# Sums of squares amid the first k chunk, an earlier fetch of the exponential's table, turns by twos and closer spatial products in a two-layer decoder trunk

## Chip, cores and metric

The kernel runs on one core of a Trainium2 chip. The metric is the device time of one execution in microseconds (us). The kernel before takes 947.1 us, the median of three runs (946.36 to 947.19).

## The reference, cut to what matters

Two layers work on 256 tokens of width 1024, in fp32. Each layer adds half of a gated feed-forward (width 2816), then a mixer, then half of a second feed-forward; every one of these starts from an RMS norm. The first layer's mixer runs dilated window attention (8 heads of 64) beside a gated spatial product (4 groups of 128), and the second layer's is causal attention with 16 heads (256 tokens are one block, so no other block is chosen).

```python
def rms_norm(x, g):
    xf = x.astype(jnp.float32)
    y = xf * lax.rsqrt(jnp.mean(xf * xf, axis=-1, keepdims=True) + EPS)
    return (y * g.astype(jnp.float32)).astype(x.dtype)

def chunked_spatial_gating(u, v, v_norm_g, w_s, b_s):
    u = jax.nn.gelu(u)
    v = rms_norm(jax.nn.gelu(v), v_norm_g)
    ...
    mixed = jnp.einsum('gpq,bnqgc->bnpgc', ws, v) + jnp.swapaxes(b_s, 0, 1)[None, None, :, :, None]
    return (u * mixed).reshape(b, s, g * c)

    # reference()
    for layer in range(DEPTH):
        h = h + 0.5 * swiglu(rms_norm(h, ffn1_norm[layer]), ...)
        hn = rms_norm(h, mix_norm[layer])
        h = h + (ab_mixer(hn, ...) if layer % 2 == 0 else c_mixer(hn, ...))
        h = h + 0.5 * swiglu(rms_norm(h, ffn2_norm[layer]), ...)
    return rms_norm(h, final_norm)
```

## The kernel before

Activations lie transposed in SBUF: features on the partitions, the 256 tokens along the row. Every product is made of three matmuls on reduced-precision operands (`mm3`, lines 223 to 226): each fp32 operand is split into a high half, written by ScalarE (`whi`, line 105; `split`, line 229), and a low half, the difference, written by VectorE (`wlo`, line 106; line 230). The matmuls are high by high (L224), high by low (L225) and low by high (L226).

Weights stream in chunks of 1 MB. `Stream` loads them over SyncE's queue into three raw buffers and splits them into four pairs of split buffers, so splits run up to four chunks ahead of TensorE. `take` hands out the next chunk, `free` gives its buffers back and starts the next loads and splits. The instructions of each engine are put in order when the program is built, by a scheduler that sees the order of the Python code; on TensorE that order is nearly the code's.

A stage doesn't wait for its norm: its matmuls run on values without the factor 1/rms, and this factor is put on behind them. `Next.pair` (lines 265 to 290) collects the squares of the new activations with VectorE adds into `acc`; `Next.sums` (line 291) adds them over the partitions with four small TensorE matmuls against ones (L295) and takes the mean (`ms`, L297, VectorE) and the root (`rstd`, L233, GpSimd). `Next.spread` turns the factor into a row that all partitions hold: two wide copies on ScalarE (L310), two TensorE instructions (L312, L313) and two copies (`row`, `half`).

Both mixers start with `first_tiles` (line 752). Its q chunk makes two tiles of 128 columns, `ps4[0]` and `ps4[1]`, with their last two k at the end; then come the sums, then the k chunk's two tiles, then the spread. `put_q` and `put_k` scale these tiles by the row and split them. The scores of two heads that lie in one tile of 128 partitions use operands of which one half of the partitions is zero (`ql0` to `ql3`); `make_attention` clears those with one memset of `zeros` (L628) and casts of it on GpSimd (L633).

Attention of a head has three parts. `scores` (line 667) runs four matmuls (L676, L677), VectorE's masked minimum (L680), the exponential on ScalarE (L683), the reciprocal of its sum (L686) and the scaling of the probabilities (L690, on GpSimd, for the last four heads on VectorE). `turn` transposes the probabilities with three TensorE instructions (L698) and splits them; `weighted` multiplies two heads by v. These parts and the spatial products (`mixing`, with a two-buffered `tmp`) are hung into the stream of weight tiles by `Slots`: `step()` is called after each tile and runs what stands at that slot. In the first mixer slots 0 to 3 are the first tiles, 4 to 7 v, 8 to 11 the gate's v, 12 to 15 its u, 16 to 19 the last q and k tiles, 20 to 27 the output projection. In the second 0 to 3 are the first tiles, and the projection has 24 to 31.

ScalarE holds one table of functions at a time. The program loads the exponential's where the exponentials of L683 follow other functions; the first mixer also needs one for the gate's gelu (L822, L859).

Of the kernel before, what the change touches and what calls it, by code (L numbers as in the profile page):

```python
# [10 lines left out]
F32 = mybir.dt.float32  # L11
F32R = mybir.dt.float32r
AF = mybir.ActivationFunctionType
ALU = mybir.AluOpType

S = 256
D = 1024
NT = S // 128
KD = D // 128
# [12 lines left out]
LINE, SHIFT = 64, 16  # L32
# [110 lines left out]
def trunk(ctx: ExitStack, tc: tile.TileContext, a, out):  # L143
    nc = tc.nc
# [3 lines left out]
    wk = ctx.enter_context(tc.tile_pool(name="wk", bufs=2))  # L148
# [10 lines left out]
    st = Stream(nc, (raw_pool, hi_pool, lo_pool))  # L159
# [463 lines left out]
    def make_attention(mp, mask_cols, nheads, v, mix, rows=False):  # L623

        qs, ks, probs, pts = {}, {}, {}, {}
        pairs, flying = (4, 5) if rows else (2, 4)
        zeros = mp.tile([128, S], F32, name="zeros")
        nc.gpsimd.memset(zeros, 0.0)  # L628
        seconds = [mp.tile([128, 2 * S + LINE], F32R, name=f"ql{i}") for i in range(pairs)]
        for t in seconds:  # L630
            for j in range(2):
                o = slice(64 - j * 64, 128 - j * 64)
                nc.gpsimd.tensor_copy(t[o, SHIFT + j * S : SHIFT + (j + 1) * S], zeros[o, :])  # L633
        mask = mp.tile([128, 384], F32, name="mask")
        nc.scalar.dma_start(mask, a["consts"][:, mask_cols])

        def scaled(bk):
            t = mp.tile([128, S], F32, name="qk", bufs=3)
            nc.vector.tensor_mul(t, bk[:, :S], norm["row"])
            return t  # L640

        def sides(j):
            return slice(j * 64, j * 64 + 64), slice(64 - j * 64, 128 - j * 64)

        def put_q(p, bk):

            t = bk[:, :S] if rows else scaled(bk)
            qq = mp.tile([128, 2 * S + LINE], F32R, name="q", bufs=pairs)
            for j in range(2):
                q, ql = (u[:, SHIFT + j * S : SHIFT + (j + 1) * S] for u in (qq, seconds[p % pairs]))  # L650
                r, o = sides(j)
                nc.scalar.activation(q[r, :], t[r, :], AF.Copy)
                nc.vector.tensor_sub(ql[r, :], t[r, :], q[r, :].bitcast(F32))
                nc.gpsimd.tensor_copy(q[o, :], q[r, :].bitcast(F32))
                qs[2 * p + j] = (q, ql)

        def put_k(p, bk):

            t = scaled(bk)
            for j in range(2):  # L660
                k = mp.tile([128, S], F32R, name=f"k{j}", bufs=pairs)
                r, o = sides(j)
                nc.scalar.activation(k[r, :], t[r, :], AF.Copy)
                nc.gpsimd.tensor_sub(k[o, :], t[r, :], k[r, :].bitcast(F32))
                ks[2 * p + j] = k

        def scores(h):
            q, ql = qs.pop(h)
            k = ks.pop(h)
            sc = bank()  # L670
            pr = mp.tile([128, 384], F32, name="pr", bufs=flying)
            nm = wk.tile([128, 2], F32, name="nm")
            l = wk.tile([128, 2], F32, name="l")
            for b in range(2):
                bs = slice(b * 128, b * 128 + 128)
                nc.tensor.matmul(sc[:, b * S : (b + 1) * S], q[:, bs], k, start=True, stop=False)  # L676
                nc.tensor.matmul(sc[:, b * S : (b + 1) * S], ql[:, bs], k, start=False, stop=True)  # L677
            for b, (c0, n) in enumerate(((0, 128), (128, 256))):
                cs = slice(c0, c0 + n)
                nc.vector.tensor_tensor_reduce(pr[:, cs], sc[:, b * S : b * S + n], mask[:, cs],  # L680
                                               norm["score"][:, b : b + 1] if rows else -SCALE, 3e38,
                                               op0=ALU.add, op1=ALU.min, accum_out=nm[:, b : b + 1])
                nc.scalar.activation(pr[:, cs], pr[:, cs], AF.Exp, bias=nm[:, b : b + 1], scale=-1.0,  # L683
                                     accum_out=l[:, b : b + 1])
            rl = wk.tile([128, 2], F32, name="rl")
            nc.vector.reciprocal(rl, l)  # L686
            for b, (c0, n) in enumerate(((0, 128), (128, 256))):
                cs = slice(c0, c0 + n)
                engine = nc.gpsimd if h < nheads - 4 else nc.vector
                engine.tensor_scalar(pr[:, cs], pr[:, cs], rl[:, b : b + 1], None, op0=ALU.mult)  # L690
            probs[h] = pr

        def turn(h):
            p, j = divmod(h, 2)
            pr = probs.pop(h)
            tp = bank()
            for i in range(3):
                nc.tensor.transpose(tp[:, i * 128 : (i + 1) * 128], pr[:, i * 128 : (i + 1) * 128], ident)  # L698
            if j == 0:
                pts[p] = [mp.tile([128, 2, 384], F32R, name=n, bufs=2) for n in ("pth", "ptl")]  # L700
            split(pts[p][0][:, j, :], pts[p][1][:, j, :], tp[:, :384])

        def weighted(p):
            o = bank().rearrange("p (j c) -> p j c", j=2)
            pth, ptl = pts.pop(p)
            vs = slice(p * 128, (p + 1) * 128)
            mm3(o, v[0][:, 0, vs], v[1][:, 0, vs], pth[:, :, :256], ptl[:, :, :256], True, False)
            mm3(o[:, :, 128:], v[0][:, 1, vs], v[1][:, 1, vs], pth[:, :, 256:], ptl[:, :, 256:], False, True)
            for j in range(2):
                r = slice(j * 64, j * 64 + 64)  # L710
                split(mix[0][r, p], mix[1][r, p], o[r, j, :].rearrange("p (t c) -> p t c", t=NT))

        return put_q, put_k, scores, turn, weighted
# [7 lines left out]
    class Slots:  # L721
# [9 lines left out]
        def step(self, *_):  # L731
            for f, i in self.events.pop(self.now, []):
                f(i)
            self.now += 1

    def tile_of(p, w, j, ks=range(KD)):

        cs = slice(j * 128, (j + 1) * 128)
        for k in ks:
            mm3(p[:, :S], w[0][k][:, cs], w[1][k][:, cs], xT["h"][:, k], xT["l"][:, k], k == 0, k == KD - 1)  # L740
# [11 lines left out]
    def first_tiles(put_q, put_k, step):  # L752

        ps4 = [bank() for _ in range(4)]
        w = st.take()
        for j, ks in LATE:
            tile_of(ps4[j], w, j, ks)
        for _ in range(2):
            step()
        st.free()  # L760
        nxt.sums()
        w = st.take()
        for j in range(2):
            tile_of(ps4[2 + j], w, j)
            step()
        nxt.spread()
        norm["score"] = wk.tile([128, NT], F32, name="score", bufs=1)
        nc.vector.tensor_scalar(norm["score"], norm["col"], -SCALE, None, op0=ALU.mult)
        for j in range(2):
            put_q(j, ps4[j])  # L770
            put_k(j, ps4[2 + j])
        st.free()
# [23 lines left out]
    def ab_mixer(phase):  # L796
        with tc.tile_pool(name="mp", bufs=1) as mp:
# [4 lines left out]
            put_q, put_k, scores, turn, weighted = make_attention(mp, slice(0, 384), 8, v, mix)  # L802
# [46 lines left out]

            slots = Slots()  # L850
            slots.at((9,), lambda _: turn_spatial())
            slots.at((15, 16, 17, 18), mixing)
            slots.at((6, 7, 8, 9, 20, 20, 21, 21), scores)
            slots.at((9, 10, 11, 12, 22, 22, 23, 23), turn)
            slots.at((13, 14, 24, 25), weighted)

            def put_u(i, p):
# [3 lines left out]
            step = slots.step  # L861
# [9 lines left out]
    def c_mixer(phase):  # L871
        with tc.tile_pool(name="mp", bufs=1) as mp:
            mix = mix_tiles(mp)
            v = v_tiles(mp, D)
            put_q, put_k, scores, turn, weighted = make_attention(mp, slice(384, 768), 16, v, mix, True)

            slots = Slots()
            slots.at((5, 6, 7, 8, 12, 13, 14, 15, 16, 17, 18, 19, 24, 24, 25, 25), scores)
            slots.at((8, 9, 10, 11, 15, 16, 17, 18, 19, 20, 21, 22, 26, 26, 27, 27), turn)
            slots.at((11, 13, 18, 20, 22, 24, 28, 29), weighted)  # L880
            step = slots.step
            for c in range(4):
                if c:
                    tiles(put_q, c, step)
                    tiles(put_k, c, step)
                else:
                    first_tiles(put_q, put_k, step)
                if c % 2 == 0:
                    token_block(lambda t, p: put_v(v, t, p, c * 256), step)
            project(mix, MIX2, phase, step)  # L890
            assert not slots.events
# [48 lines left out]
```

## Time and profile before

| | us |
|---|---|
| median of the runs | 947.1 |
| the profiled execution's own time | 947.28 |
| its span in the trace | 945.6 |
| first mixer's sums of squares, start | 196.0 |
| first mixer's output projection, last matmuls | near 284 |
| second mixer's sums of squares, start | 651.3 |
| second mixer's output projection, last matmuls | near 757 |

A row of the page or of a view names the line, the engine and the instruction, what it writes and reads, and its shape. In a timeline the first number is the start in us from the span's start, the second the duration, and a bracket at the end holds the idle time of the engine in front of it and what ended that. `x3` stands for three such instructions in a row. In the chain of waits each row is a piece of the chain that ended last.

### The profile page before, as it was taken

How to read it: one execution, taken by the hardware profiler on the slowest of the kernel's cores; microseconds unless marked ns; L12 is line 12 of the kernel's file. 1: busy time of each engine (PE TensorE's matmuls, PEld its weight loads, DVE VectorE, ACT ScalarE, POOL GpSimd, SP SyncE). 2: the span in 40 equal slices, each digit the busy share in tenths (PEclk: the TensorE clock that was granted, in tenths of full speed). 3: DMA queues.
4: the chain of work that ended last, by engine and by line, in shares of the span. 5: the costliest groups of instructions: out<-in, count | busy, mean ns of one | idle time of the engine just before them, and what ended most of it. 6: DMA issues, size and time to landing. Idle time of an engine off the chain costs nothing.

```text
span 945.6 us, 18144 instructions
## 1 busy us (share of the span) xinstructions
PE 935.2 (99%) x7685; PEld 912.3 (96%) x7685; DVE 609.2 (64%) x879; ACT 502.2 (53%) x787; POOL 93.5 (10%) x116
## 2 busy tenths in 40 slices
PE   9999999999999999999999999999999999999997
PEld 8999999988999999999999999999999999999886
DVE  6766656677876665655765665567787865665543
ACT  7745444468676544444554544455786755544431
POOL 0000000034400000000000000004684000000000
PEclk9999999999999999999999999999999999999999
DMA  9866555665446656656756655656544476555521
GB/s 295 286 193 207 169 187 182 224 220 178 135 134 199 202 180 198 193 158 210 223 180 183 208 189 169 199 185 214 175 138 135 134 221 202 178 180 200 202 89 44
DMA packets 153537, 174.86 MB, mean 185 GB/s; under 512 B 3008, under 2 KB 142192, under 8 KB 153456
## 3 DMA queue, kind: packets, MB, share of 16 engines
q1 hardware_dynamic: 151888, 171.54, 56.7%
q10 hardware_dynamic: 1568, 2.17, 0.7%
q8 instruction: 60, 0.98, 0.4%
q14 instruction: 21, 0.17, 0.0%
HBM read 172.65 MB, written 1.05 MB: 184 GB/s over the span
## 4 chain that ended last, share of the span: by engine, by line
PE 91%; DVE 5%; ACT 2%; issue 1%; DMA 1%; POOL 0%; SPq 0%; POOLq 0%; ACTq 0%
PE bank L225 28%; PE bank L224 28%; PE bank L226 28%; DVE wlo L106 2%; PE bank L549 2%; PE bank L546 2%; PE bank L545 2%; PE bank L698 1%; DMA raw<-in_ffn_w_gate 1%; PE bank L677 0%; PE bank L676 0%; ACT whi L105 0%; DVE xTl L262 0%; PE bank L295 0%; POOL rsg L233 0%
## 5 line engine op out<-in xcount | busy, mean ns | idle before, releaser
L105 ACT ACTIVATE whi<-raw 128x1024 fp32r<-128x1024 f32 (+4 forms) x352 | 331.2, 985 | 369.8 <-issue 287.5
L106 DVE TENSOR_TENSOR wlo<-raw,whi 128x1024 fp32r<-128x1024 f32 (+4 forms) x352 | 390.7, 1142 | 132.4 <-ACT whi L105 131.3
L224 PE MATMUL bank<-xTh,whi 128*128 128x256 f32 x1632 | 453.1, 278 | 0.0
L225 PE MATMUL bank<-xTl,whi 128*128 128x256 f32 x1632 | 451.6, 277 | 0.2 <-DVE xTl L262 0.2
L226 PE MATMUL bank<-xTh,wlo 128*128 128x256 f32 x1632 | 451.3, 277 | 0.2 <-DVE wlo L106 0.2
L225 PEld LDWEIGHTS bank<-xTl,whi 128*128 128x128 f32 x1632 | 306.4, 188 | 0.9 <-DVE xTl L262 0.8
L226 PEld LDWEIGHTS bank<-xTh,wlo 128*128 128x128 f32 x1632 | 306.6, 188 | 0.6 <-DVE wlo L106 0.6
L224 PEld LDWEIGHTS bank<-xTh,whi 128*128 128x128 f32 x1632 | 306.4, 188 | 0.1
L224 PE MATMUL bank<-hTh,whi 128*128 128x256 f32 x528 | 145.7, 276 | 0.0
L225 PE MATMUL bank<-hTl,whi 128*128 128x256 f32 x528 | 145.7, 276 | 0.0
L226 PE MATMUL bank<-hTh,wlo 128*128 128x256 f32 x528 | 145.7, 276 | 0.0
L226 PEld LDWEIGHTS bank<-hTh,wlo 128*128 128x128 f32 x528 | 99.1, 188 | 0.0
L224 PEld LDWEIGHTS bank<-hTh,whi 128*128 128x128 f32 x528 | 99.1, 188 | 0.0
L225 PEld LDWEIGHTS bank<-hTl,whi 128*128 128x128 f32 x528 | 99.1, 188 | 0.0
L486 DVE TENSOR_TENSOR hm<-gs,bank 128x512 f32<-128x512 f32 x44 | 30.2, 688 | 80.0 <-PE bank L226 79.6
L483 DVE TENSOR_TENSOR gs<-bank,row 128x512 f32<-128x512 f32 x44 | 30.0, 690 | 47.7 <-PE bank L226 47.7
L224 PE MATMUL bank<-mixh,whi 128*128 128x256 f32 x128 | 35.3, 281 | 0.0
L225 PE MATMUL bank<-mixl,whi 128*128 128x256 f32 x128 | 35.1, 277 | 0.0
L226 PE MATMUL bank<-mixh,wlo 128*128 128x256 f32 x128 | 35.0, 277 | 0.0
L628 POOL MEMSET zeros<- 128x256 f32 x2 | 0.6, 312 | 341.9 <-DVE x L273 341.9
L690 POOL TENSOR_SCALAR pr<-pr,rl 128x128 f32<-128x128 f32 (+1 forms) x32 | 32.9, 1041 | 15.4 <-DVE rl L686 15.1
L233 POOL TENSOR_TENSOR rstd<-ms,half_neg 128x2 f32<-128x2 f32 x6 | 5.1, 851 | 269.3 <-DVE ms L297 252.6
(139 smaller groups left out, 908.7 us busy)
## 6 DMA issues: line engine op xcount, KB each, us to landing
raw<-in_ffn_w_gate SPq DMA_DIRECT2D x42, 1024.0 KB, 5.3
raw<-in_ffn_w_up SPq DMA_DIRECT2D x42, 1024.0 KB, 5.4
raw<-in_ffn_w_down SPq DMA_DIRECT2D x35, 1024.0 KB, 5.1
raw<-in_c_w_in SPq DMA_DIRECT2D x12, 1024.0 KB, 5.2
raw<-in_ab_w_in SPq DMA_DIRECT2D x10, 1024.0 KB, 5.2
raw<-in_ffn_w_down SPq DMA_DIRECT2D x12, 768.0 KB, 4.4
raw<-in_ab_w_out SPq DMA_DIRECT2D x4, 1024.0 KB, 5.1
raw<-in_c_w_out SPq DMA_DIRECT2D x4, 1024.0 KB, 5.0
```

The source lines that it names most:

```text
L105: nc.scalar.activation(hi, r, AF.Copy)
L106: nc.vector.tensor_sub(lo, r, hi.bitcast(F32))
L224: nc.tensor.matmul(p, sh, mh, start=start, stop=False)
L225: nc.tensor.matmul(p, sh, ml, start=False, stop=False)
L226: nc.tensor.matmul(p, sl, mh, start=False, stop=stop)
L483: nc.vector.tensor_mul(g, both(pg), twice(norm["row"]))
L486: nc.vector.tensor_mul(hm, g, both(pu))
L545: nc.tensor.matmul(banks[t, h], sh, w[0][kw][:, cs], start=k == 0, stop=False)
L546: nc.tensor.matmul(banks[t, h], sh, w[1][kw][:, cs], start=False, stop=False)
L549: nc.tensor.matmul(banks[t, h], sl, w[0][kw][:, cs], start=False, stop=k == FT - 1)
L690: engine.tensor_scalar(pr[:, cs], pr[:, cs], rl[:, b : b + 1], None, op0=ALU.mult)
L698: nc.tensor.transpose(tp[:, i * 128 : (i + 1) * 128], pr[:, i * 128 : (i + 1) * 128], ident)
```

## The change

Five edits, all in the mixers:

- `make_attention` clears the zero halves with memsets of their own; the tile `zeros` (1 KB a partition) and the casts are gone.
- `put_k` runs an exponential of one element a partition, into a spare `l`, behind the second pair of k in both mixers, and behind the fourth (last) pair in the first mixer.
- `first_tiles` computes the first four k of the k chunk's second tile, then the sums, then the first tile, then the rest of the second.
- the spatial products move from slots 15, 16, 17, 18 to 15, 16, 16, 17.
- the turns of two heads share a slot, the later one's: 9, 10, 11, 12 become 10, 10, 12, 12 in the first mixer, and 8 to 11 and 15 to 22 become 9, 9, 11, 11 and 16, 16 to 22, 22 in the second.

```diff
@@ make_attention
-        zeros = mp.tile([128, S], F32, name="zeros")
-        nc.gpsimd.memset(zeros, 0.0)
         seconds = [mp.tile([128, 2 * S + LINE], F32R, name=f"ql{i}") for i in range(pairs)]
         for t in seconds:
             for j in range(2):
                 o = slice(64 - j * 64, 128 - j * 64)
-                nc.gpsimd.tensor_copy(t[o, SHIFT + j * S : SHIFT + (j + 1) * S], zeros[o, :])
+                nc.gpsimd.memset(t[o, SHIFT + j * S : SHIFT + (j + 1) * S].bitcast(F32), 0.0)
@@ put_k
                 ks[2 * p + j] = k
+            if p == 1 or p == 3 and not rows:
+
+                nc.scalar.activation(wk.tile([128, 2], F32, name="l")[:, :1], t[:, :1], AF.Exp, scale=0.0)
@@ first_tiles
         st.free()
+        w = st.take()
+        tile_of(ps4[3], w, 1, range(4))
         nxt.sums()
-        w = st.take()
-        for j in range(2):
-            tile_of(ps4[2 + j], w, j)
-            step()
+        tile_of(ps4[2], w, 0)
+        step()
+        tile_of(ps4[3], w, 1, range(4, KD))
+        step()
         nxt.spread()
@@ ab_mixer
-            slots.at((15, 16, 17, 18), mixing)
+            slots.at((15, 16, 16, 17), mixing)
             slots.at((6, 7, 8, 9, 20, 20, 21, 21), scores)
-            slots.at((9, 10, 11, 12, 22, 22, 23, 23), turn)
+            slots.at((10, 10, 12, 12, 22, 22, 23, 23), turn)
@@ c_mixer
             slots.at((5, 6, 7, 8, 12, 13, 14, 15, 16, 17, 18, 19, 24, 24, 25, 25), scores)
-            slots.at((8, 9, 10, 11, 15, 16, 17, 18, 19, 20, 21, 22, 26, 26, 27, 27), turn)
+            slots.at((9, 9, 11, 11, 16, 16, 18, 18, 20, 20, 22, 22, 26, 26, 27, 27), turn)
```

## The prediction, made before the changed kernel ran

> **What bounds the kernel now.** I read the page first, then the waits of PE, then PE's timeline at each of them, and last the other engines' timelines there.
>
> ```profile
> span 945.6 us, 18144 instructions
> PE 935.2 (99%) x7685; PEld 912.3 (96%) x7685; DVE 609.2 (64%) x879; ACT 502.2 (53%) x787; POOL 93.5 (10%) x116
> PE 91%; DVE 5%; ACT 2%; issue 1%; DMA 1%; POOL 0%; SPq 0%; POOLq 0%; ACTq 0%
> ```
>
> The page's first lines and its chain of waits: PE sets the time. The change adds no matmul and removes none, so it can only win time in which PE stands still. The waits view of PE says where (total, times, longest, in us):
>
> ```profile
> PE bank L295 <- DVE acc L289: 1.4, 2, 0.8
> ...
> PE bank L698 <- DVE pr L690: 0.7, 1, 0.7
> PE bank L676 <- POOL k L664: 0.2, 1, 0.2
> ```
>
> These are the waits inside the mixers: the sums of squares (L295) once in each mixer, the last turn of probabilities (L698), and a score (L676). A busy PE can hide part of a stall, because matmuls overlap, so I take it from the starts in PE's timeline (start, duration, instruction):
>
> ```profile
> 195.14 0.28 PE L226 MATMUL bank<-xTh,wlo 128*128 128x256 f32 x1
> 196.00 0.58 PE L295 MATMUL bank<-ones,acc 128*128 128x1 f32 x4 [0.58 <-DVE acc L289]
> ...
> 650.17 0.28 PE L225 MATMUL bank<-xTl,whi 128*128 128x256 f32 x1
> 650.28 0.28 PE L226 MATMUL bank<-xTh,wlo 128*128 128x256 f32 x1
> 651.34 0.58 PE L295 MATMUL bank<-ones,acc 128*128 128x1 f32 x4 [0.78 <-DVE acc L289]
> ```
>
> Matmuls of 256 columns start 0.11 us apart (650.17, 650.28). The sums start 0.86 us after their predecessor in the first mixer and 1.06 us in the second: 0.75 and 0.95 us lost.
>
> The first mixer loses more at its end. Rows of PE, ACT, DVE and POOL there:
>
> ```profile
> 260.35 0.28 PE L226 MATMUL bank<-mixh,wlo 128*128 128x256 f32 x1
> 260.88 0.39 PE L676 MATMUL bank<-k,q 128*128 128x256 f32 x1 [0.25 <-POOL k L664]
> ...
> 268.38 0.49 PE L698 MATMUL bank<-ident,pr 128*128 128x128 f32 x3
> 269.58 0.61 PE L698 MATMUL bank<-ident,pr 128*128 128x128 f32 x3 [0.70 <-DVE pr L690]
> 257.91 1.06 ACT L105 ACTIVATE whi<-raw 128x1024 fp32r<-128x1024 f32 x1
> 260.52 1.28 ACT L683 ACT_TABLE_LOAD   x1 [1.54 <-DVE nm L680]
> 261.81 0.40 ACT L683 ACTIVATE pr<-pr,nm 128x128 f32<-128x128 f32 x1
> 259.01 1.23 DVE L106 TENSOR_TENSOR wlo<-raw,whi 128x1024 fp32r<-128x1024 f32 x1 [0.61 <-ACT whi L105]
> 262.84 0.17 DVE L686 RECIPROCAL rl<-l 128x2 f32<-128x2 f32 x1 [1.50 <-ACT pr L683]
> 257.20 1.80 POOL L848 TENSOR_TENSOR mixl<-tmp,mixh 128x256 fp32r<-128x256 f32 x1
> 259.08 2.55 POOL L664 TENSOR_TENSOR k<-qk,k 64x256 fp32r<-64x256 f32 x2
> ```
>
> PE loses 0.53 - 0.11 = 0.42 us before the score and 1.20 - 3 x 0.11 = 0.87 us before the last turn: 1.29 us in all. The score waits for k's low halves on POOL (259.08), which stand behind the last spatial product's low half (257.20). The turn waits for a chain over ACT and DVE; in it DVE idles 1.50 us for the first exponential, which the table load (1.28 us) held up.
>
> **The change part by part.** *Sums of squares amid the k chunk.* Twelve matmuls (four k of the second tile) now run ahead of the sums: 12 x 0.11 = 1.3 us of cover against waits of 0.75 and 0.95. The order of instructions in the built program confirms those twelve on PE. What reads the sums gets them later, and DVE's order puts two weight splits between the last sum and the mean (L297), where there were none. The rows of the first mixer:
>
> ```profile
> 192.00 2.43 POOL L633 CAST ql<-zeros 64x256 fp32r<-64x256 f32 x4
> 193.56 0.62 DVE L289 TENSOR_TENSOR acc<-acc,sq 128x256 f32<-128x256 f32 x1
> 195.34 2.01 ACT L105 ACTIVATE whi<-raw 128x1024 fp32r<-128x1024 f32 x2 [2.05 <-PE bank L225]
> 195.44 0.41 DVE L289 TENSOR_TENSOR acc<-acc,sq 128x256 f32<-128x256 f32 x1
> 196.92 0.71 POOL L233 TENSOR_TENSOR rstd<-ms,half_neg 128x2 f32<-128x2 f32 x1 [2.48 <-DVE ms L297]
> 197.67 0.70 ACT L310 ACTIVATE wide<-ones,rstd 128x128 f32<-128x128 f32 x2 [0.31 <-POOL rstd L233]
> 197.74 2.36 DVE L106 TENSOR_TENSOR wlo<-raw,whi 128x1024 fp32r<-128x1024 f32 x2
> 201.99 0.28 PE L312 MATMUL bank<-ident,wide 128*128 128x128 f32 x1
> ```
>
> The splits need ACT's two halves (195.34 to 197.35), so they end near 197.4 + 1.2 = 198.6 (half of 2.36 for one). Mean, root and wide copies with their hand-overs take 1.8 us now, from the sums' end (196.00 + 0.58) to 197.67 + 0.70 = 198.37, and bring this to about 200.4. The spread (L312), at 201.99 now, comes 0.75 us earlier, at 201.2. Slack 0.8 us, where it was 3.6: nothing is lost, but little is left. Gain: 0.75 and 0.95.
>
> Does it last? In the second mixer the waits view has no further wait of PE behind the sums until the projection, so 0.95 lasts. In the first, the chain of waits runs on PE until the fourth head is turned, and then over the other engines to the last turn:
>
> ```profile
> 230.53 0.34 PE bank L698 x3
> 230.89 0.50 ACT pth L229
> ```
>
> That chain starts when PE turns, so an earlier PE moves it as a whole. I carry 0.75 through.
>
> *Zeros.* Two memsets and twelve casts on POOL become twelve memsets. While casts run, DVE's add takes 0.62 us (193.56), just behind them 0.41 (195.44). The casts thus lengthen what the sums wait for; now that these are covered, this is worth nothing more on PE. The memsets are bounded above by the cast (2.43 / 4 = 0.61 us), below by nothing; only scores read the zeros, behind the spread. Taken: 0. The tiles behind the removed 1 KB a partition move in SBUF; no row prices that, and I take nothing for it.
>
> *Exponential's table.* Three dummy exponentials (second k pair of both mixers, last k pair of the first) draw the three loads of L683 forward; there are as many loads as before. In the first mixer's end the load moves from 260.52 to behind the k copies, near 257.9, in front of a split. ACT idles 1.54 us before the load now, so its time there is free, but the split (257.91) and DVE's half of it (259.01, for which DVE already waits 0.61) come later by 1.28 and the dummy; the dummy is bounded by nothing and by the 0.40 us of an exponential with 64 times the elements in a row, taken 0.2. DVE's order has the first head's scores in front of that half now. So DVE's wait of 1.50 goes, and up to 1.28 + 0.2 = 1.48 comes back in front of the split: between 1.29 us gained (all of PE's wait) and 1.48 lost, nearest to zero. The two fetches behind the first k pairs count nothing: no wait of PE follows there before 260.35 in the first mixer, and none but the projection's in the second.
>
> In a sentence by itself: the Trainium skill, "ScalarE: Activation LUTs", section "What ACT_TABLE_LOAD costs", says that a switch takes the load's 1283 ns and a drain of some 1380 ns behind it. The trace disagrees: the exponential starts at 261.81, 0.01 us after the load's end. By that rule the moved load would push the split by 1.38 us more, 945.2 + 1.4 = 946.6; the rival of a standstill below is its case.
>
> *Spatial products closer.* The last two products (each with two matmuls, and DVE, ACT and POOL work) move one weight tile earlier, 24 x 0.11 = 2.6 us. The last one's POOL part (1.80) leaves the place in front of k's low halves, which is worth up to the 0.42 us that the score waits. Against it, their DVE adds now stand in front of a q copy, and the two buffers of `tmp` make DVE wait for POOL. With the table I take 0.2 us for the end of the first mixer, out of the bounds of 1.29 gained and 1.48 lost.
>
> *Turns by twos.* One turn and a pair of turns on PE, each with the matmul behind it:
>
> ```profile
> 673.28 0.49 PE L698 MATMUL bank<-ident,pr 128*128 128x128 f32 x3
> 673.72 0.28 PE L225 MATMUL bank<-xTl,whi 128*128 128x256 f32 x1
> ...
> 738.34 0.82 PE L698 MATMUL bank<-ident,pr 128*128 128x128 f32 x6
> 739.12 0.28 PE L225 MATMUL bank<-mixl,whi 128*128 128x256 f32 x1
> ```
>
> One costs 0.44 - 0.11 = 0.33 us, two at once 0.78 - 0.11 = 0.67, so eight pairs in place of sixteen turns save 8 x (0.66 - 0.67), which is nothing. No turn comes before its old slot, so none waits longer for its probabilities.
>
> Sum: 0.75 + 0.95 + 0.2 = 1.9 us. The profiled execution took 947.28 us, 1.7 more than its span of 945.6; 947.28 - 1.9 = 945.4. The median of the runs shown is 947.1, 0.2 lower, so I predict 945.2.
>
> **Rivals.** *The first mixer's end loosens altogether.* Score and turn no longer wait: 0.75 + 0.95 + 1.29 = 3.0, 944.1. For it: the two causes named in the rows (load, low half on POOL) are both moved. Against it: DVE and ACT have no less work there, and splits take the freed place.
>
> *Only the second mixer gains.* The first one's end is set by DVE work that doesn't move with PE, or the spread, with its 0.8 us of slack, takes over the sums' wait: 0.95, 946.15. For it: the end's chain is not PE's.
>
> *The change doesn't do what it says* (the sums' wait turns up whole at the spread in both mixers): 947.1.
>
> *A standstill behind the load*, as long again as the load (1.28 us), in front of the split: 945.2 + 1.3 = 946.5. Against it: 0.01 us between the load and the exponential at 261.81.
>
> *Slower: a fetch in ACT's way.* ACT runs in order, so what stands behind each dummy waits 1.48 us. If at all three places the split behind it is what DVE and then PE need next, 3 x 1.48 = 4.4 us is lost against 1.7 gained: 949.8. It decides once the splits run less than 1.5 us ahead of PE. For it: DVE waits for a split of ACT at 259.01. Against it: PE itself has no wait for a split in the mixers' part of the waits view.
>
> **How the numbers follow.** About 0.2%, 1.9 us here, is what a measurement of this kernel can tell from no change; the forecast lies on that line. The forecast 0.48, with its own range of 944.6 to 945.8 (0.25 beyond the line, 0.23 within it); loosened 0.30, since PE's waits there have their named causes moved; only the second mixer 0.12; no effect 0.02; standstill 0.01; slower 0.07. Faster 0.25 + 0.30 = 0.55, within 0.2% 0.23 + 0.12 + 0.02 + 0.01 = 0.38, slower 0.07. The range reaches from just beyond the loosened end, 943.7, to just short of no change, 946.8.
>
> **What would show it.** Right: no wait at L295 in either mixer; the spread without a wait in front of it; a table load right behind the k copies and none in front of the last four heads' exponentials; first scores of those heads not waiting for POOL; about 0.33 us a head for turns as before. Wrong: PE waiting at the spread, at the first scores of the last four heads or on a weight split, or a longer wait before the last turn than 0.87 us.

## The result, and the profile after

The changed kernel takes 945.23 us (median of 20 runs, 944.62 to 946.23). The kernel before, timed beside it, takes 946.5 us (20 runs, 946.02 to 947.54; the three runs of 947.1 shown earlier lie inside that). The ratio is 0.9987, 95% interval 0.9981 to 0.9993: 1.2 us faster, between 0.7 and 1.8. The execution profiled took 944.62 us, the lowest of its twenty. Executions at a lower granted clock are left out of the ratios; the profiled one of e4 below is among them (971.53 us at 0.948), so of e4 no trace is read.

The page's first lines of the changed kernel, and the waits view of its TensorE (PE):

```profile
span 942.9 us, 18152 instructions
PE 933.5 (99%) x7685; PEld 911.5 (97%) x7685; DVE 607.5 (64%) x879; ACT 502.1 (53%) x790; POOL 83.4 (9%) x114
```

```profile
PE bank L699 <- DVE pr L691: 1.3, 1, 1.3
PE bank L399 <- DVE warm L392: 1.1, 1, 1.1
PE bank L225 <- DVE xTl L262: 0.3, 1, 0.3
PE bank L226 <- DVE wlo L106: 0.2, 1, 0.2
```

The waits for the sums (L295) and for the score are gone. The wait for the last turn (L698, now L699) has grown from 0.7 to 1.3 us. GpSimd (POOL) is busy 10.1 us less. Of this 4.1 us come from the clearing (7.2 us of casts and 0.6 us of `zeros` memsets became 3.7 us of memsets); 5.4 us come from the scaling of the probabilities (32.9 to 27.5 us for the same 32 instructions), of which the turns by twos alone (e5) and the fetch alone (e6) each show about half.

PE's timeline at the sums of both mixers, with the spread of the first (start, duration, instruction):

```profile
195.42 0.28 PE L226 MATMUL bank<-xTh,wlo 128*128 128x256 f32 x1
195.54 0.50 PE L295 MATMUL bank<-ones,acc 128*128 128x1 f32 x4
195.90 0.37 PE L224 MATMUL bank<-xTh,whi 128*128 128x256 f32 x1
...
198.68 0.69 ACT L310 ACTIVATE wide<-ones,rstd 128x128 f32<-128x128 f32 x2 [2.40 <-POOL rstd L233]
199.98 0.28 PE L226 MATMUL bank<-xTh,wlo 128*128 128x256 f32 x1
200.10 0.27 PE L312 MATMUL bank<-ident,wide 128*128 128x128 f32 x1
...
649.75 0.28 PE L226 MATMUL bank<-xTh,wlo 128*128 128x256 f32 x1
649.87 0.50 PE L295 MATMUL bank<-ones,acc 128*128 128x1 f32 x4
650.23 0.37 PE L224 MATMUL bank<-xTh,whi 128*128 128x256 f32 x1
```

The sums now start 0.12 us behind their predecessor, as any matmul does, and no bracket of idle time is left. The wide copies end at 198.68 + 0.69 = 199.37, the spread starts at 200.10 right behind the matmul at 199.98: 0.73 us of slack, and no wait.

The end of the first mixer, on PE, ScalarE (ACT), VectorE (DVE) and POOL:

```profile
254.47 0.28 PE L226 MATMUL bank<-mixh,wlo 128*128 128x256 f32 x1
254.76 0.39 PE L677 MATMUL bank<-k,q 128*128 128x256 f32 x1
...
265.89 0.49 PE L699 MATMUL bank<-ident,pr 128*128 128x128 f32 x3
267.68 0.61 PE L699 MATMUL bank<-ident,pr 128*128 128x128 f32 x3 [1.29 <-DVE pr L691]
256.11 1.28 ACT L666 ACT_TABLE_LOAD   x1
257.41 0.20 ACT L666 ACTIVATE l<-qk 128x1 f32<-128x1 f32 x1
257.52 1.05 ACT L105 ACTIVATE whi<-raw 128x1024 fp32r<-128x1024 f32 x1
258.47 0.38 ACT L684 ACTIVATE pr<-pr,nm 128x128 f32<-128x128 f32 x1
258.60 1.22 DVE L106 TENSOR_TENSOR wlo<-raw,whi 128x1024 fp32r<-128x1024 f32 x1 [1.43 <-ACT whi L105]
261.56 0.17 DVE L687 RECIPROCAL rl<-l 128x2 f32<-128x2 f32 x1 [0.67 <-ACT pr L684]
255.73 2.28 POOL L662 TENSOR_TENSOR k<-qk,k 64x256 fp32r<-64x256 f32 x2 [0.22 <-ACT k L661]
```

The table load stands at 256.11, behind the k copies, and the exponential at 258.47 needs none. But DVE's idle 1.50 us in front of the reciprocal has become 1.43 us in front of the split that waits for ACT behind the load. And though POOL writes k's low halves sooner and the score hardly waits (0.29 us from start to start, 0.53 before), the last turn waits longer.

### Where the time went

Both traces hold the same 7164 weight-type matmuls (L224 to L226), so the n-th of one can be set against the n-th of the other. The table gives how much shorter (minus) or longer each kernel makes four stretches than the kernel before, worked out from these starts. The stretches start and end at the same matmuls: the first mixer's sums (192.1 to 205.1 us of the trace before), the rest of that mixer to behind its last turn (to 272.1), the second mixer's sums (649.0 to 655.1), and the rest of that mixer to its last turns (to 740.0).

| kernel | ratio to before, 95% interval | 1st sums | rest of 1st | 2nd sums | rest of 2nd |
|---|---|---|---|---|---|
| changed | 0.9987 (0.9981 to 0.9993) | -0.80 | -0.01 | -1.04 | +0.33 |
| changed, second time (e9) | 0.9984 (0.9975 to 0.9993) | -0.80 | +0.01 | -1.04 | +0.33 |
| zeros alone (e1) | 0.9987 (0.9978 to 0.9996) | -0.61 | +0.04 | -0.85 | 0.00 |
| moved sums alone (e2) | 0.9983 (0.9975 to 0.9992) | -0.80 | +0.04 | -1.04 | +0.22 |
| zeros and moved sums (e3) | 0.9985 (0.9976 to 0.9993) | -0.78 | +0.08 | -1.04 | +0.01 |
| turns by twos alone (e5) | 0.9994 (0.9985 to 1.0003) | +0.04 | -0.48 | -0.01 | +0.33 |
| fetch alone (e6) | 0.9998 (0.9989 to 1.0007) | +0.05 | +0.01 | -0.01 | 0.00 |
| closer products alone (e7) | 1.0006 (0.9997 to 1.0015) | +0.02 | +0.55 | -0.01 | +0.10 |
| changed, more resets (e8) | 0.9983 (0.9974 to 0.9992) | -0.81 | +0.01 | -0.92 | +0.39 |
| changed, old products (e10) | 0.9980 (0.9971 to 0.9989) | -0.80 | -0.45 | -1.04 | +0.33 |
| changed, 2nd turns singly (e11) | 0.9982 (0.9973 to 0.9991) | -0.80 | 0.00 | -1.04 | 0.00 |
| zeros, sums, 1st turns by twos (e12) | 0.9977 (0.9968 to 0.9986) | -0.81 | -0.47 | -1.04 | 0.00 |

Between these stretches, where the code is the same, traces differ by up to 0.4 us. In the first 28 us they differ by up to 0.7 us, and the changed kernel's first trace by 1.08. This scatter is why single parts of 0.3 us are read from the stretches and not from the times. A single trace can be off inside a stretch too (+0.22 in e2's second mixer, where no edit explains it), so the parts put down to turns and products are each taken from more than one trace.

The change's own sum is -0.80 - 0.01 - 1.04 + 0.33 = -1.52 us; the runs' two ratios say 1.2 and 1.5.

### The profile page after: what moved, and what is told of

It is laid out like the page before. It is cut to its first block, busy times and chain, and to the rows that moved or that the text cites. A ratio compares the mean times of both kernels' runs of the same rounds, so it can differ in the third digit from the quotient of the medians.

```text
span 942.9 us, 18152 instructions
## 1 busy us (share of the span) xinstructions
PE 933.5 (99%) x7685; PEld 911.5 (97%) x7685; DVE 607.5 (64%) x879; ACT 502.1 (53%) x790; POOL 83.4 (9%) x114
## 4 chain that ended last, share of the span: by engine, by line
PE 69%; DVE 2%; ACT 1%; issue 1%; POOLq 0%; POOL 0%; ACTq 0%
PE bank L224 21%; PE bank L225 21%; PE bank L226 20%; PE bank L545 2%; PE bank L549 2%; PE bank L546 2%; DVE wlo L106 1%; PE bank L699 1%; PE bank L677 0%; PE bank L678 0%; ACT whi L105 0%; DVE xTl L262 0%; PE bank L475 0%; DVE pr L691 0%; DVE pr L681 0%
## 5 line engine op out<-in xcount | busy, mean ns | idle before, releaser
L224 PE MATMUL bank<-xTh,whi 128*128 128x256 f32 x1632 | 452.5, 277 | 0.0
L226 PE MATMUL bank<-xTh,wlo 128*128 128x256 f32 x1632 | 451.2, 276 | 0.2 <-DVE wlo L106 0.2
L226 PEld LDWEIGHTS bank<-xTh,wlo 128*128 128x128 f32 x1632 | 306.4, 188 | 0.6 <-DVE wlo L106 0.4
L224 PEld LDWEIGHTS bank<-xTh,whi 128*128 128x128 f32 x1632 | 306.5, 188 | 0.2 <-ACT whi L105 0.2
L224 PE MATMUL bank<-hTh,whi 128*128 128x256 f32 x528 | 145.7, 276 | 0.0
L226 PE MATMUL bank<-hTh,wlo 128*128 128x256 f32 x528 | 145.7, 276 | 0.0
L226 PEld LDWEIGHTS bank<-hTh,wlo 128*128 128x128 f32 x528 | 99.1, 188 | 0.0
L224 PEld LDWEIGHTS bank<-hTh,whi 128*128 128x128 f32 x528 | 99.1, 188 | 0.0
L224 PE MATMUL bank<-mixh,whi 128*128 128x256 f32 x128 | 35.2, 280 | 0.0
L226 PE MATMUL bank<-mixh,wlo 128*128 128x256 f32 x128 | 35.0, 277 | 0.0
L631 POOL MEMSET ql<- 64x256 f32 x12 | 3.7, 309 | 342.1 <-DVE x L273 341.7
L546 PE MATMUL bank<-wlo,hTh 128*128 128x512 f32 x80 | 31.1, 389 | 0.0
L545 PE MATMUL bank<-whi,hTh 128*128 128x512 f32 x80 | 31.1, 389 | 0.0
```

The costliest lines, as they stand in the source:

```text
L224: nc.tensor.matmul(p, sh, mh, start=start, stop=False)
L226: nc.tensor.matmul(p, sl, mh, start=False, stop=stop)
L545: nc.tensor.matmul(banks[t, h], sh, w[0][kw][:, cs], start=k == 0, stop=False)
L546: nc.tensor.matmul(banks[t, h], sh, w[1][kw][:, cs], start=False, stop=False)
L631: nc.gpsimd.memset(t[o, SHIFT + j * S : SHIFT + (j + 1) * S].bitcast(F32), 0.0)
```

## The experiments

### Which edit took the wait at the sums

e1 has the zeros edit alone:

```diff
-        zeros = mp.tile([128, S], F32, name="zeros")
-        nc.gpsimd.memset(zeros, 0.0)
...
-                nc.gpsimd.tensor_copy(t[o, SHIFT + j * S : SHIFT + (j + 1) * S], zeros[o, :])
+                nc.gpsimd.memset(t[o, SHIFT + j * S : SHIFT + (j + 1) * S].bitcast(F32), 0.0)
```

> The kernel before with the zeros edit alone: the sums of squares stand where they stood, right behind the q chunk. Theory A (the prediction's: the sums were late by their place in the code, and the zeros are worth nothing on TensorE): both waits at L295 stay, 0.75 and 0.95 us by the starts, and the time is that of before, within 0.3 us. Rival B (the casts on GpSimd made the sums late by slowing VectorE's adds and split, 0.62 against 0.42 us an add): the last adds take 0.42 us and end 0.6 us earlier in the first mixer and 0.95 us earlier in the second, so that the waits at L295 are at most 0.2 us each, and the time falls by 1.3 to 1.6 us, near the whole change's.

e2 has the moved sums alone, e3 both edits:

```diff
         st.free()
-        nxt.sums()
         w = st.take()
-        for j in range(2):
-            tile_of(ps4[2 + j], w, j)
-            step()
+        tile_of(ps4[3], w, 1, range(4))
+        nxt.sums()
+        tile_of(ps4[2], w, 0)
+        step()
+        tile_of(ps4[3], w, 1, range(4, KD))
+        step()
```

> The kernel before with the sums moved behind the first four k of the second tile, and nothing else. Theories A and B both: no wait at L295, as the twelve matmuls (1.3 us) cover 0.75 and 0.95; the casts still run and the adds still take 0.62 us. A gain of 1.7 us if the spread doesn't wait; if it takes over a part of the wait (splits at 1.4 us each and two of them in front of the mean), PE shows a wait at L312 and the gain is less by that much.

> The kernel before with the zeros edit and the moved sums. Theory A: as the moved sums alone, 1.7 us under before. Rival B: the two edits pay for the same waits, so it is no more than 0.3 us under the better of the two single ones. If the whole change gives back some 0.3 us by its turns, this kernel is that much faster than the whole change, which had 0.9987 of before.

Medians beside a before of 947.0: e1 945.68, e2 945.31, e3 945.43. Each edit alone gives nearly the whole gain, and both together give no more. Timelines of e1, the sums where they were:

```profile
191.99 1.37 POOL L631 MEMSET ql<- 64x256 f32 x4 [171.81 <-DVE x L273]
193.60 0.43 DVE L289 TENSOR_TENSOR acc<-acc,sq 128x256 f32<-128x256 f32 x1
195.07 0.42 DVE L289 TENSOR_TENSOR acc<-acc,sq 128x256 f32<-128x256 f32 x1
195.41 0.28 PE L226 MATMUL bank<-xTh,wlo 128*128 128x256 f32 x1
195.64 0.58 PE L295 MATMUL bank<-ones,acc 128*128 128x1 f32 x4
196.08 0.36 PE L224 MATMUL bank<-xTh,whi 128*128 128x256 f32 x1
```

Beside the casts (0.61 us each) the first add took 0.62 us; beside memsets (0.34 us each) it takes 0.43. From the matmul ahead of the sums to the one behind them PE now needs 0.67 us (195.41 to 196.08), where it needed 1.30 before (195.14 to 196.44) and needs 0.48 in the changed kernel (195.42 to 195.90). The row behind the sums in the timeline of before:

```profile
196.44 0.36 PE L224 MATMUL bank<-xTh,whi 128*128 128x256 f32 x1
```

So rival B holds: the casts made the sums late, and the zeros alone remove 0.61 + 0.85 of the 0.80 + 1.04 us. The place of the sums in the code was a second way to the same gain. e1's time fits (0.9987, 1.3 us).

### The single parts of the rest

e5 has the turns by twos alone, e6 the three dummy exponentials, e7 the closer products.

```diff
-            slots.at((9, 10, 11, 12, 22, 22, 23, 23), turn)
+            slots.at((10, 10, 12, 12, 22, 22, 23, 23), turn)
...
-            slots.at((8, 9, 10, 11, 15, 16, 17, 18, 19, 20, 21, 22, 26, 26, 27, 27), turn)
+            slots.at((9, 9, 11, 11, 16, 16, 18, 18, 20, 20, 22, 22, 26, 26, 27, 27), turn)
```

> The kernel before with the turns by twos, and nothing else. Theory C (the prediction's: eight pairs cost what sixteen singles cost, 0.67 against 0.33 us): the time of before; the matmuls of the second mixer between its sums and its projection start as far behind the sums as before, within 0.1 us. Rival D (a single turn ends a slow run of matmuls, 0.1178 against 0.1133 us, and a pair with two heads' products behind it leaves one): runs of 24 or more slow matmuls behind the pairs near 683, 686 and 717 us, and the projection comes 0.25 to 0.35 us later against the sums than before; the time rises by 0.3 us, at the edge of what the runs can tell, so the trace decides. The waits at L295 stay.

```diff
+            if p == 1 or p == 3 and not rows:
+
+                nc.scalar.activation(wk.tile([128, 2], F32, name="l")[:, :1], t[:, :1], AF.Exp, scale=0.0)
```

> The kernel before with the three dummy exponentials, and nothing else. Prediction's share for the end of the first mixer: between 1.29 us gained and 1.48 lost, near zero. Theory E (the fetch moves VectorE's standstill and does not shorten it): VectorE's idle time of 1.50 us in front of the reciprocal is gone, and an idle time of 1.3 to 1.9 us stands in front of the split's second half; the wait in front of the last turn is 0.7 to 1.4 us, and the projection starts within 0.3 us of where it did against the first mixer's sums. Rival F (the fetch frees the last turn, and only the closer products or the turns gave it back in the whole change): the wait in front of the last turn is under 0.3 us and the end of the first mixer 0.5 us or more earlier. The two fetches behind the first pairs show no wait of TensorE behind them.

```diff
-            slots.at((15, 16, 17, 18), mixing)
+            slots.at((15, 16, 16, 17), mixing)
```

> The kernel before with the last two spatial products one weight tile earlier, and nothing else. Theory E: the first score of the last heads no longer waits (0.42 us by the starts falls under 0.2), but the last turn, which hangs on the table load and the exponentials, comes at most 0.2 us earlier, so that its wait grows by what the score gave and the projection starts within 0.2 us of where it did. Rival G (the closer products carry the whole share that was predicted for the end): the projection starts 0.3 to 0.5 us earlier against the sums.

*Turns.* Rival D holds in the second mixer: its rest takes 0.33 us more. But the first mixer becomes 0.48 us shorter, which no theory had. The rows that show where that begins, in the timelines of the kernel before:

```profile
227.90 0.47 ACT L229 ACTIVATE pth<-bank 128x384 fp32r<-128x384 f32 x1
228.27 1.68 ACT L105 ACTIVATE whi<-raw 128x384 fp32r<-128x384 f32 x2
229.98 1.49 DVE L106 TENSOR_TENSOR wlo<-raw,whi 128x1280 fp32r<-128x1280 f32 x1 [0.46 <-ACT whi L105]
231.39 0.16 DVE L828 TENSOR_SCALAR msg<-ssg 128x4 f32<-128x4 f32 x1
238.67 1.21 DVE L106 TENSOR_TENSOR wlo<-raw,whi 128x1024 fp32r<-128x1024 f32 x1
```

The same work in e5, and its last turn:

```profile
227.51 2.11 ACT L105 ACTIVATE whi<-raw 128x384 fp32r<-128x384 f32 x3 [0.15 <-PE bank L226]
229.65 1.49 DVE L106 TENSOR_TENSOR wlo<-raw,whi 128x1280 fp32r<-128x1280 f32 x1 [0.55 <-ACT whi L105]
230.59 0.87 ACT L229 ACTIVATE pth<-bank 128x384 fp32r<-128x384 f32 x2 [0.69 <-PE bank L698]
231.06 0.16 DVE L828 TENSOR_SCALAR msg<-ssg 128x4 f32<-128x4 f32 x1
238.00 1.22 DVE L106 TENSOR_TENSOR wlo<-raw,whi 128x1024 fp32r<-128x1024 f32 x1
269.12 0.50 PE L698 MATMUL bank<-ident,pr 128*128 128x128 f32 x2 [0.70 <-DVE pr L690]
```

Before, ACT copies the third head's turn (`pth`, 0.47 us) between pieces of a weight split; with pairs there is nothing to copy there, and the split ends 0.33 us earlier (DVE's half starts at 229.65 instead of 229.98). Behind that split DVE takes the mean square of the gate's norm (`msg`, L828), 1.41 us after the split's start in both kernels (231.39 and 231.06). From there the chain of waits runs over POOL, DVE and ACT to the last turn, not over PE, and all of it moves. By 245 us the lead has grown to 0.46 us (a split that starts at 245.60 before starts at 245.14 in e5). In between, the split of 238.67 (238.00 in e5) and a low half of `mixl` have changed places on DVE; whether that order made the further 0.13 us isn't shown. The last turn, at 269.58 before, starts at 269.12 in e5, again 0.46 us earlier.

*Fetch.* Theory E holds. DVE's timeline of e6, the split behind the load and the next wait:

```profile
259.75 1.32 DVE L106 TENSOR_TENSOR wlo<-raw,whi 128x1024 fp32r<-128x1024 f32 x1 [1.42 <-ACT whi L105]
262.81 0.17 DVE L689 RECIPROCAL rl<-l 128x2 f32<-128x2 f32 x1 [0.67 <-ACT pr L686]
```

The standstill of 1.50 us moved in front of the split (1.42) and 0.67 is left in front of a reciprocal. The score's wait went and the last turn's wait grew to 1.3 us; the stretch is as long as before (+0.01). Rival F does not hold.

*Products.* Neither theory: they cost 0.55 us. The first score still waits (0.4 us in e7's waits view). Timelines of the kernel before:

```profile
249.23 0.42 ACT L847 ACTIVATE mixh<-tmp 128x256 fp32r<-128x256 f32 x1 [1.13 <-DVE tmp L845]
249.55 1.05 ACT L105 ACTIVATE whi<-raw 128x1024 fp32r<-128x1024 f32 x1
250.63 1.23 DVE L106 TENSOR_TENSOR wlo<-raw,whi 128x1024 fp32r<-128x1024 f32 x1 [0.71 <-ACT whi L105]
```

The same in e7, whose PE runs 0.52 us ahead there by its start:

```profile
249.11 0.42 DVE L845 TENSOR_TENSOR tmp<-tmp,uT 128x256 f32<-128x256 f32 x1
249.57 0.42 ACT L847 ACTIVATE mixh<-tmp 128x256 fp32r<-128x256 f32 x1 [0.44 <-DVE tmp L845]
249.90 1.05 ACT L105 ACTIVATE whi<-raw 128x1024 fp32r<-128x1024 f32 x1
250.18 0.49 DVE L844 TENSOR_TENSOR tmp<-bank,sbias 128x128 f32<-128x128 f32 x2 [0.30 <-POOL mixl L848]
250.98 1.23 DVE L106 TENSOR_TENSOR wlo<-raw,whi 128x1024 fp32r<-128x1024 f32 x1 [0.31 <-ACT whi L105]
269.61 0.50 PE L698 MATMUL bank<-ident,pr 128*128 128x128 f32 x2 [1.32 <-DVE pr L690]
```

The third product has moved ahead of the weight split that starts on ACT at 249.55 before. Its adds and its multiply (L844, L845) run on DVE first, ACT's copy of the result (`mixh`, L847, at 249.57) waits 0.44 us for them, and the split stands behind that copy. With the 0.52 us added, ACT's split comes at 250.42 (249.55 before), DVE's at 251.50 (250.63), both 0.87 us later, and the last turn at 270.13 (269.58). A product is missing further on, so of 0.87 us 0.55 is left at the end. DVE also waits 0.30 us for POOL to give back a buffer of `tmp` (250.18). That wait costs nothing here: behind it DVE still idles 0.31 us for ACT's half of the split.

### Turns one by one, and more resets

e4 is the changed kernel with all turns at their old slots, the inverse of e5's edit. e8 is the changed kernel with all q and k chunks of the second mixer stored in halves for their first three k:

```diff
-        add_cols(wc, c * 256, 256, reset=RESET if c % 2 else 0)
-        add_cols(wc, 1024 + c * 256, 256, reset=0 if c else RESET)
+        add_cols(wc, c * 256, 256, reset=RESET)
+        add_cols(wc, 1024 + c * 256, 256, reset=RESET)
```

> The changed kernel with the turns at their old slots, all else as changed. Theory C (a pair of turns costs what two singles cost): the time of the changed kernel, 0.9987 of before, within 0.15 us. Rival D (TensorE's matmuls run in runs of a faster and a slower pace, 0.1133 and 0.1178 us for 256 columns; a single turn ends a slow run, and with pairs slow runs of 24 to 49 matmuls are left in the second mixer): 0.3 us faster than the changed kernel, 1.5 to 1.7 us under before, and the milestones of the second mixer's tiles come 0.3 us earlier against its sums.

> The changed kernel with one thing added: all q and k weight chunks of the second mixer have their first three k stored in halves, as half of these chunks have already. The same products are summed in matmuls of other shapes there, and nothing is left out. Rival D: where such a chunk starts behind a pair, the slow run ends after a few matmuls; the runs of 24 to 49 slow matmuls are gone, and the projection of the second mixer starts 0.25 to 0.35 us earlier against its sums than in the changed kernel; the time is 0.3 us under the changed one's if the halves themselves cost nothing. Theory C: no slow runs that hang on the turns, so no change, or a loss by what the halves cost.

e4 took 945.92 us beside 947.0, ratio 0.9990 (0.9981 to 0.9999): not 0.3 us faster than the changed kernel. By the single parts it gains 0.33 us in the second mixer and loses 0.48 in the first, which fits, but the times alone don't show it; the traces of e11 (second mixer) and e12 (first mixer) do. e8 missed. The changed kernel has three stretches at a slower matmul pace in the second mixer, 26, 24 and 49 matmuls long (shown below). In e8 the first two are gone, but the third is still 31 long (715.1 us), a new one of 50 stands behind the next pair of turns (722.4 us), and the rest of that mixer takes 0.39 us more than before instead of nothing more. Halves of a chunk move such stretches and do not remove them. Its ratio (0.9983) can't be told from e9's (0.9984).

### Combinations, side by side on one chip

e9 is the changed kernel again. e10 puts the products back to slots 15 to 18, e11 the second mixer's turns to their old slots. e12 is the kernel before with zeros, moved sums and the first mixer's turns by twos:

```diff
-            slots.at((9, 10, 11, 12, 22, 22, 23, 23), turn)
+            slots.at((10, 10, 12, 12, 22, 22, 23, 23), turn)
```

> The changed kernel once more, on the chip and beside the runs of the three kernels that follow, so that they can be set against it. 1.3 to 1.7 us under before. The slow runs of matmuls behind the pairs of turns in the second mixer (26, 24 and 49 long) stand at the same places as in its first trace if they hang on the order of the matmuls, and elsewhere if they are chance.

> The changed kernel with the spatial products at their old slots 15, 16, 17, 18. Theory H (by the single edits: the closer products put their adds, with a wait for GpSimd's tmp buffer, in front of the weight splits on which the end of the first mixer hangs, and cost 0.56 us there; the turns by twos give 0.49 us there; the fetch nothing): 0.5 us faster than the changed kernel, the last turn's wait shorter by as much. Rival (the parts are not additive: with the fetch in place the old products hold up k's low halves, and the score's wait comes back): within 0.2 us of the changed kernel, with a wait at the first score of the last heads.

> The changed kernel with the turns of the second mixer one by one at their old slots, those of the first mixer by twos. Rival D: no slow run of 20 matmuls or more between the second mixer's sums and its last turns, and the projection 0.3 us earlier against the sums; 0.3 us faster than the changed kernel. Theory C: within 0.1 us of it.

> The kernel before with the zeros edit, the moved sums, and the turns by twos in the first mixer alone; products, turns of the second mixer and the table's loads as before. Sum of the single edits by the traces: 0.83 + 1.04 for the sums, 0.49 for the turns of the first mixer, 2.36 in all, so 944.6 where before is at 947.0, and 0.8 us under the changed kernel. If the parts are not additive it is no faster than the moved sums alone (0.9983 of before).

Medians beside a before of 946.71: e9 945.20, e10 944.95, e11 944.83, e12 944.53. The stretches do what the single parts said, each within 0.05 us: old products shorten the first mixer by 0.46 us (theory H said 0.5; the wait of the last turn, though, stays at 1.3, since PE too arrives earlier), single turns take the 0.33 us out of the second, e12 has both. The stretches at the slower pace in e9 are again 26, 24 and 49 matmuls long, at the same matmuls, so they hang on the order of matmuls and aren't chance. PE's timeline has one of them in the changed kernel's first trace (first and last start, 49 matmuls apart):

```profile
714.38 0.28 PE L225 MATMUL bank<-ptl,vth 128*128 128x256 f32 x1
...
720.15 0.28 PE L226 MATMUL bank<-xTh,wlo 128*128 128x256 f32 x1
```

The same place in e11, behind a single turn (first and last start at the faster pace, 23 matmuls apart):

```profile
715.39 0.28 PE L224 MATMUL bank<-xTh,whi 128*128 128x256 f32 x1
...
717.99 0.28 PE L226 MATMUL bank<-xTh,wlo 128*128 128x256 f32 x1
```

5.77 / 49 = 0.1178 us against 2.60 / 23 = 0.1130. Every row says 0.28 us, and the granted clock is 1.00 in both: only the starts show it. The three stretches together make 99 x 0.0048 = 0.47 us, more than the 0.33 us lost in that mixer; where the pairs win back the rest was not followed.

e12 is the fastest kernel: 0.9977 (0.9968 to 0.9986), 2.2 us under before and 0.67 us by the medians under the changed kernel, where the stretches say 0.8. The intervals of e9 and e12 overlap, so the times alone don't separate these two; the stretches do. The one wait of its PE inside the mixers, from the waits view:

```profile
PE bank L696 <- DVE pr L688: 0.7, 1, 0.7
```

## Why the prediction was right, and where its steps were not

The forecast was 945.2 us and the median is 945.23, but the gain was 1.9 by the sum and is 1.2 to 1.5 by the runs: the sum was made against 947.1, and the runs of before that stand beside the result have 946.5. That the forecast meets the median to 0.03 us is luck: a gain forecast some 0.6 us too large and a starting point 0.6 us too high cancel. Term by term:

- *Sums, 0.75 and 0.95.* Right; 0.80 and 1.04. The sums and the next matmul's start also take 0.36 us (195.54 to 195.90) where they took 0.44 behind a standstill, and that was left out. The spread kept the slack forecast for it: 0.73 us, 0.8 forecast.
- *Zeros, nothing more on PE.* Right beside the moved sums (e3 against e2). The prediction saw that casts slow VectorE's adds and did not draw the conclusion that this was most of the wait: alone, the zeros bring 0.61 + 0.85 (e1).
- *Fetch.* The bounds of 1.29 gained and 1.48 lost were right, and the value near zero: 0.01 alone. What goes at the reciprocal comes back at the split, as the prediction wrote. The load took the 1.28 us and the dummy the 0.20 us taken for them (the exponential used as its bound has 128 times its elements in a row, not 64).
- *Closer products.* This step failed. It weighed 0.42 us for the score against adds "in front of a q copy" and a wait for `tmp`'s buffers, and took the first for the larger. The adds are the larger: with the multiply and ACT's copy that hang on them they stand in front of a weight split too and put it off by 0.87 us, of which 0.55 us is lost at the end (e7; 0.46 by e10 against e9). The wait for the buffer is there (0.30 us) but hidden, so theory H is right on the adds and not on this wait. With the fetch a gain of 0.2 was carried; both alone measure 0.56 lost.
- *Turns by twos, nothing.* This step failed twice, and the two errors nearly cancel. It priced the turns on PE alone, start to start. In the first mixer, ACT's copy of the odd head left the middle of a weight split on the chain that sets the mixer's end: 0.48 us gained. The prediction had read this chain as starting from the fourth head's turn on PE (`pth` at 230.89). In e5 the copies of that turn (230.59 + 0.87 = 231.46) still run when `msg` starts at 231.06, so the chain hangs on the split. In the second, where the prediction looked no further than the one matmul behind a pair, matmuls further on run at the slower pace in stretches of 26, 24 and 49: 0.33 us lost. So time was also lost where PE never stands still, which the prediction had ruled out as a place to win.
- *The end of the first mixer, 0.2.* It came out at 0.01 as the sum of 0.48 gained, 0.01 and 0.55 lost, which the single runs show to be additive (+0.08 against -0.01).

Of the signs named as right, all are there but one: the table load, the spread, the sums, POOL out of the score's way; 0.33 us a head holds for the turns themselves but not for what runs behind them. Of those named as wrong, one came true: the wait before the last turn is 267.68 - 265.89 - 0.34 = 1.45 us, more than 0.87. It cost nothing, since PE got there that much earlier while the other engines' chain came out even.

Of the rivals, the first mixer's end did not loosen altogether (e12 shortens it by 0.47 us, without fetch and products). The fetch in ACT's way did not come: e6 shows no wait of PE for a weight split in either mixer. No standstill follows the load: the dummy starts at 257.41, 0.02 us behind the load's end (256.11 + 1.28). Nor is there one ahead of it: the k copies in front of it end at 256.09. The drain of some 1380 ns that the Trainium skill states in "ScalarE: Activation LUTs", section "What ACT_TABLE_LOAD costs", isn't seen here either.

## What to carry to other kernels

When two edits aim at one wait, run each alone: here clearing tiles by memset rather than by cast removed most of a wait that had been put down to the place of its consumer. An edit that is priced on the busiest engine alone can still move the chain that ends a stage on the others; find that chain's start and ask whether the edit adds or removes work in front of it. Gains of a few tenths are read from stretches between the same instructions in two traces, as the times scatter by as much in code that nobody touched.

## What the runs showed of the hardware

VectorE's add with two operands from SBUF takes 0.62 us while GpSimd casts from SBUF and 0.41 to 0.43 us while it writes memsets or rests; the weight split takes 1.41 us beside casts and 1.22 us beside memsets (194.11 in e2's trace, 192.59 in the changed kernel's). The Trainium skill, "SBUF — State Buffer", section "Who interferes with whom", states it so: a VectorE instruction with two SBUF inputs contends with a GpSimd instruction that reads SBUF, not with one that only writes. The runs agree, and add the size, some 0.2 us for each.

TensorE's 256-column matmuls start at two paces, 0.113 and 0.118 us apart, at a granted clock of 1.00, and the second can last for dozens of them. In four executions with turns by twos in the second mixer (changed, e5, e9, e10) the same three stretches at the slower pace appear behind pairs of turns; in the eight traces with single turns there, only e7's has one of 20 or more between the sums and the last turns (23, from 673.8 us). That mixer's other changes of pace, +0.22 in e2, have no edit to hang on. What sets the pace is not known; chunks stored in halves move such stretches and do not remove them (e8).
